# Trainium2: a hybrid attention, mLSTM and convolution layer: another issue order in the first quarter, another ring for the residual loads, other durations in the order's estimate

## The chip, the cores and the metric

One core of one Trainium2 chip runs the whole kernel. TensorE (PE) does matmuls and transposes, VectorE (DVE), ScalarE (ACT) and GpSimd (POOL) the elementwise work, and every transfer is issued by one DMA queue, that of SyncE (SP). The metric is the time of one execution on the device in microseconds (us), over which the median of several runs is taken.

## The reference

x is 2048 tokens by 1024 channels, and there is one layer. One input projection feeds three groups, and one output projection mixes them and adds the residual:

```python
h = rms_norm(x, norm_g)
a_q, a_k, a_v, a_z, m_q, m_k, m_v, m_o, m_z, m_i, m_f, c_a, c_b, c_z = split_columns(h @ w_in)

att = chunk_band_attention(a_q, a_k, a_v, ...)         # 4 heads of 64, chunks of 64 tokens, 8 chunks back
att = att * silu(a_z)

m_q, m_k = silu(causal_depthwise_conv([m_q, m_k], width 4))
hm = mlstm_chunkwise(m_q, m_k, m_v, m_i + b_i, m_f + b_f)   # 4 heads of 128, state carried over tokens
ml = rms_norm(sigmoid(m_o) * hm) * silu(m_z)

u = c_a * sigmoid(c_b)                                  # 256 channels
u = causal_depthwise_conv(u, width 31)
cv = silu(layer_norm(u)) * silu(c_z)

out = x + concat(att, ml, cv) @ w_out
```

## The kernel before, in words

The sequence is worked in four quarters of 512 tokens (`NQ`, `TQ`). In each quarter every projection is a *unit*: `kv`, `qg` (queries and gate inputs), `v`, `o`, then `mk`, `mq`, `z` of mLSTM heads 0 to 3, `az` and `cz` (gates of attention and convolution), `cb` and `ca` (inputs of the convolution), and `out0` to `out7`. A unit with the tokens along the free side (`cm`) is 24 matmuls of 128x512: 8 blocks of channels times 3 passes, since each product is made of rounded high and low parts. A unit like `v` has 96 of them. Names in a row tell the unit: `pmm_az` is the PSUM bank of an `az` unit.

In the first quarter a piece of weights comes raw (`rw`), ACT casts it and POOL (sometimes DVE) makes the low part (`w<-rw,w`); the pair is kept in DRAM (`wk`) and later quarters load it from there (`w<-wk`). The ring of weight tiles has 10 (`WB`).

The small work hangs on *chains*, Python generators that emit instructions on all engines. While the program of a unit is written, the chains that are due are advanced between its matmuls. What is due is decided by an estimate: `Engine`, `dma`, `mm` and `tp` keep a clock for each engine, and `pace`, `tick` and `wait_for` read it. The estimate fixes the order of instructions once, when the kernel is built. On the chip each engine runs its own list in that order, and so does the DMA queue, in which a transfer that must wait holds back those behind it. The list of units is fixed by hand: `FIRST` + `TAIL` for quarter 0, `LATER` + `TAIL` for the others, and eight `out` units of the last quarter at the end (`order_of`). The `out` units of a quarter run at the head of the next quarter's list.

Chains that the prediction speaks of:
- the gates chain: from the eight gate inputs (`gt`) VectorE makes log-sigmoids with a polynomial of eight small steps (`gpp<-gpp,gz`); then PE transposes the result (`ptg<-ident_r,gt`), while `v` units fill PE;
- a head of the mLSTM: after `mk` and `mq`, four taps of a short convolution on DVE (`macc<-mraw,mcw_t,macc` three times, and `macc<-mraw,macc` behind the SiLU), then transposes `pk`, scores `pS<-macc`, and for each of four blocks three products `pp` (numerator with `kw`, with `dt`, and with the state `cst`);
- the attention: scores `pss`, softmax on DVE (`pr<-pss`), transposes `ptp`, products `po`;
- the convolution: 62 taps a quarter on DVE (`cvu<-cvu,cvw_t`), and behind the last tap the layer norm by blocks (`ptl` on PE, `bst`, `bmv` and `cvu<-ptl,bmv,brs` on DVE, `brs` on POOL), then transposes back (`pty`);
- the gates `az`, `z`, `cz` (`gate`, `att_gate`), two to three DVE steps behind each unit;
- the next quarter's input: x comes transposed in eight pieces (`xk<-in_xT`), DVE scales one (`xk<-xk,gx,rb`), ACT rounds it, DVE makes the low part (`xT<-xk,xT`); the first `cb` unit of the quarter reads the eight pairs in turn;
- the end of an `out` unit (`finish`): the residual `xr` (`fetch_x`, `fetching`), an addition on DVE (`xr<-pmm_out,xr`), a store.

SBUF slots are rings by tag (`SLOTS`): X, W, H, A, B and others; a chain that wants a slot waits for the oldest of that ring.

Of the kernel before, what the change touches and what calls it, by code (L numbers as in the profile page):

```python
# [10 lines left out]
F32R = mybir.dt.float32r  # L11
# [4 lines left out]
P = 128  # L16
S = 2048
D = 1024
# [10 lines left out]
LAG = 4  # L29
DEPTH = 3  # L30

SLOTS = {"X": (5, 512), "W": (4, 528), "H": (5, 512), "A": (2, 512), "M": (1, 516), "Q": (1, 768), "B": (2, 256), "R": (3, 640),
         "T": (2, 640)}
TAP = 1.0
SEM = 0.12
# [4 lines left out]
        + [("qg", TM, 4), ("v", TM, 8), ("o", TM, 8)]  # L40
        + [(f"{n}{h}", CM, 2) for n in ("mk", "mq", "z") for h in range(4)]
        + [(f"{n}{j}", CM, 2) for n in ("az", "cz") for j in range(2)] + [(f"out{i}", CM, 2) for i in range(8)])
FIRST = ["kv", "cb0", "ca0", "cb1", "ca1", "qg", "v", "mk0", "mq0", "o", "mk1", "mq1"]
LATER = ["out0", "out1", "out2", "out3", "cb0", "ca0", "kv", "out4", "cb1", "ca1", "qg", "out5", "v", "mk0", "mq0", "o",
         "out6", "mk1", "mq1", "out7"]
TAIL = ["z0", "mk2", "mq2", "z1", "mk3", "mq3", "az0", "az1", "z2", "cz0", "cz1", "z3"]
KIND = {n: k for n, k, _ in PLAN}
PIECES = {}
_at = 0
# [5 lines left out]


def order_of(q):
    return [f"out{i}" for i in range(8)] if q == NQ else (LATER if q else FIRST) + TAIL


LOG = None
# [3 lines left out]
def kernel(ctx: ExitStack, tc: tile.TileContext, x, xT, wp, wq, norm_g, qg, kg, bias, far,  # L65
# [3 lines left out]

    free = {"V": 0.0, "A": 0.0, "G": 0.0, "D": 0.0}  # L70
    wrote, read, grain = {}, {}, {}

    class Pool:

# [171 lines left out]
    class Engine:  # L246
# [3 lines left out]
        def __getattr__(self, name):  # L250
            fn = getattr(self.eng, name)

            def call(*a, **k):
                i = tc.keep_in_program_order(fn(*a, **k))  # L254
                aps = [v for v in a if isap(v)]
                out_ = [k["out"]] if "out" in k else aps[:1]
                aps = aps if "out" in k else aps[1:]
                acc = [k["accum_out"]] if isap(k.get("accum_out")) else []
                ins = aps + [v for n_, v in k.items() if n_ not in ("out", "accum_out") and isap(v)]
                n = max([size(ap) for ap in out_ + ins if not any(st_ == 0 for st_, c_ in ap.ap[1:])] or [1])  # L260
                two = sum(1 for ap in ins if size(ap) * 2 > n) > 1 or any(ap.space == bass.MemoryType.PSUM for ap in ins)
                if self.key == "A":
                    d = 0.17 + 0.00085 * n + 0.1 * isap(k.get("scale")) + 0.08 * isap(k.get("bias")) + 0.19 * bool(acc)
                elif self.key == "V":
                    d = (0.16 + 0.00104 * n if two else 0.14 + 0.00056 * n) + 0.09 * bool(acc)
                    d += 0.05 * any(isap(k.get(x)) for x in ("scalar", "scalar1", "scalar2"))
                elif k.get("op") == ALU.pow:
                    d = 1.0
                else:
                    d = 0.25 + (0.0021 * n if two else 0.0)  # L270
                end = max(free[self.key], rdy(*ins), busy(*out_)) + d
                free[self.key] = end
                for ap in ins:
                    was_read(ap, end)
                for ap in out_ + acc:
                    was_written(ap, end + SEM)
                return i
            return call
# [3 lines left out]
    def dma(out, in_):  # L282
        start = max(clk["t"], rdy(in_), busy(out), free["D"])
        free["D"] = start + 4 * size(out) * out.shape[0] / 330e3
        was_read(in_, free["D"] + 1.0)
        was_written(out, free["D"] + 2.2)
        tc.keep_in_program_order(nc.sync.dma_start(out=out, in_=in_))

    def stall(t, what):
# [12 lines left out]

    def mm(out_, lhsT, rhs, start, stop, share=1.0):
        n = size(rhs)
        run_pe(out_, (lhsT, rhs), 0.006 + 0.00043 * n if lhsT.dtype == F32R else share * 2 * (0.004 + n / 1200.0))
        tc.keep_in_program_order(PE.matmul(out_, lhsT=lhsT, rhs=rhs, start=start, stop=stop))  # L306

    def tp(out_, in_, n=P):
        rnd = in_.dtype == F32R
        run_pe(out_, (in_,), 0.062 if rnd else 0.11)  # L310
        tc.keep_in_program_order(PE.transpose(out=out_, in_=in_, identity=(ident_r if rnd else ident)[0:n, 0:n]))  # L311


# [248 lines left out]

    def x_block(b, t, rs, xt):
        yield (rs[:, b:b + 1],)
        dg = yield from take("dg", P)
        A.activation(out=dg, in_=ident, func=AF.Copy, scale=rs[:, b:b + 1])
        yield (dg,)
        c = slice(b * P, (b + 1) * P)
        for hk in range(2):
            xb = (yield from take("xb", 512)).rearrange("p (a b) -> p a b", a=4)  # L570
            yield from bank_wait()
            pt, pt_ = bank("pxt")
            for k in range(4):
                mm(pt[:, k, :], t[:, (4 * hk + k) * P:(4 * hk + k + 1) * P], dg, True, True)
            ks = slice(4 * hk, 4 * hk + 4)
            V.tensor_tensor(out=xb, in0=pt, in1=gx[:, ks].unsqueeze(2).to_broadcast([P, 4, P]), op=ALU.mult)
            shut(pt_)
            yield (xb,)
            A.copy(out=xt[:, 0, ks, c], in_=xb)
            yield (xt[:, 0, ks, c],)  # L580
            V.tensor_tensor(out=xt[:, 1, ks, c], in0=xb, in1=f(xt[:, 0, ks, c]), op=ALU.subtract)
            drop(xb)
        drop(dg)
        done.add((0, b))
# [98 lines left out]
        return cs  # L683

    def q_chain(q, b, ps, gt, items, deps):
        raw = yield from take("qr", 256, tag="B")
        A.copy(out=raw, in_=ps[:, 0:256])
        V.tensor_tensor(out=gt[:, :, b], in0=ps[:, 256:264], in1=gb_t, op=ALU.add)
        ps_done(ps)
        box["gt"] = box.get("gt", 0) + 1  # L690
        yield from norm_heads(raw, "q")
        n3 = raw.rearrange("p (h d) -> p h d", d=64)
        V.tensor_tensor(out=n3, in0=n3, in1=gqk.unsqueeze(1).to_broadcast([P, 4, 64]), op=ALU.mult)
        yield (raw,)
        stk = (yield from take("qstk", 768, F32R, "Q")).rearrange("p (a b) -> p a b", a=4)
        A.copy(out=stk[:, :, 0:64], in_=n3)
        yield (stk,)
        V.tensor_tensor(out=stk[:, :, 64:128], in0=n3, in1=f(stk[:, :, 0:64]), op=ALU.subtract)
        V.tensor_copy(out=stk[:, :, 128:192], in_=f(stk[:, :, 0:64]))
        drop(raw)  # L700
        yield (stk,)
        while not all(c["done"] for c in deps) or len(items) > 5:
            yield 0.3
        qT = []
        for v_ in range(2):
            t = (yield from take(f"qT{v_}", 512, F32R)).rearrange("p (a b) -> p a b", a=4)
            yield from bank_wait()
            pt, pt_ = bank("ptq", F32R)
            for h in range(4):
                tp(pt[:, h, :], stk[:, h, 64 * v_:64 * v_ + P])  # L710
            A.copy(out=t, in_=pt)
            shut(pt_)
            qT.append(t)
        drop(stk)
        items.extend([(b, h, qT) for h in range(4)])
# [446 lines left out]


    def out_unit(i):
        fetch_x(i)
        ps = cm(box["mt"][0], f"out{i}", box["mt"][2])
        step(spawn(finish(i, ps, box["mt"][1])))

    def fetch_x(i):
        spawn(fetching(i, box["mt"][1]))  # L1170

    def fetching(i, q):
        xr = yield from take("xr", 512)
        yield max(0.0, busy(xr) - clk["t"])
        dma(out=xr, in_=xT[i * P:(i + 1) * P, q * TQ:(q + 1) * TQ])
        box["xr", q, i] = xr
# [7 lines left out]
    for q in range(NQ):  # L1184
# [129 lines left out]
```

## Time and profile before

| | |
|---|---|
| Median of 3 runs | 1225.51 us (1222.08 to 1225.66) |
| Profiled execution, its own time | 1225.23 us |
| Its span, first to last instruction | 1223.5 us |
| Granted TensorE clock, mean | 0.987 of full speed |
| PE / DVE / ACT / POOL busy | 96% / 65% / 35% / 20% of the span |
| Bytes moved | 240.25 MB, 196 GB/s over the span |

Some 1.7 us of the execution's time lie outside its span. A busy share tells how long an engine had something to do; an engine's idle time matters only if the chain of work that ended last runs through it. Here PE has 48.3 us of idle time in all, so the views to read are the one that names what PE waited for, and the one that gives busy time stretch by stretch.

### The profile page before, as it was taken

What the parts mean: (1) busy time and instruction counts of PE and PEld (TensorE: products, weight loads), DVE (VectorE), ACT (ScalarE), POOL (GpSimd) and SP (SyncE); (2) the same over time, 40 slices, a digit from 0 to 9 for tenths busy, and PEclk for the clock granted to TensorE, in tenths of its full rate; (3) what the DMA queues carried; (4) which work ended last, traced back from release to release, by engine and by line L of the source; (5) the groups of instructions that cost most, each with busy time, mean ns of one, the idle gap of its engine ahead of it and who ended that gap; (6) DMA issues with size and microseconds to landing.
All of it is one profiled execution on the core that took longest, in us unless ns stands there. A gap on an engine that the chain in (4) does not pass through costs nothing.

```text
span 1223.5 us, 17647 instructions
## 1 busy us (share of the span) xinstructions
PE 1175.2 (96%) x6308; PEld 967.1 (79%) x6308; DVE 797.7 (65%) x1845; ACT 430.3 (35%) x984; POOL 244.9 (20%) x325
## 2 busy tenths in 40 slices
PE   6988996999999999999899999999999999999998
PEld 5776775777778888888678888888877888888886
DVE  6386897985567577775456666767537666677731
ACT  4454633443323441334232343233312244223320
POOL 5572543560222011110022100001002200010200
PEclk9998998999999999999999999999999999999999
DMA  9583856767673417655936351855674615275463
GB/s 354 187 312 118 313 175 240 240 219 266 234 277 121 176 67 259 206 158 170 325 109 238 122 191 35 289 178 170 195 266 152 223 46 208 91 255 187 154 218 111
DMA packets 95408, 240.25 MB, mean 196 GB/s; under 512 B 11288, under 2 KB 28248, under 8 KB 95320
## 3 DMA queue, kind: packets, MB, share of 16 engines
q1 hardware_dynamic: 95320, 239.11, 57.2%
q8 instruction: 50, 0.82, 0.3%
q14 instruction: 38, 0.31, 0.1%
HBM read 186.52 MB, written 52.56 MB: 195 GB/s over the span
## 4 chain that ended last, share of the span: by engine, by line
PE 79%; DVE 9%; DMA 5%; POOL 3%; issue 2%; ACT 2%; SPq 0%; POOLq 0%; ACTq 0%; DVEq 0%
PE pmm_out L306 12%; PE pmm_v L306 7%; PE pmm_o L306 7%; PE pmm_mk L306 6%; PE pmm_mq L306 6%; PE pmm_z L306 6%; PE pmm_cz L306 4%; PE pp L306 3%; PE pmm_kv L306 3%; PE pmm_az L306 3%; PE po L306 3%; PE pmm_qg L306 3%; PE pmm_ca L306 3%; PE pss L306 3%; DVE cvu L254 3%; PE ptp L311 3%
## 5 line engine op out<-in xcount | busy, mean ns | idle before, releaser
L254 DVE SCALAR_TENSOR_TENSOR cvu<-cvu,cvw_t 128x512 f32<-128x512 f32 x240 | 193.1, 805 | 10.6 <-ACT cvu L254 6.9
L306 PE MATMUL pmm_out<-mT,w 128*128 128x512 f32 x768 | 189.2, 397 | 1.4 <-ACT mT L254 1.2
L306 PEld LDWEIGHTS pmm_out<-mT,w 128*128 128x128 f32 x768 | 141.6, 188 | 31.6 <-ACT mT L254 1.4
L254 POOL TENSOR_TENSOR w<-rw,w 128x512 fp32r<-128x512 f32 (+1 forms) x80 | 116.2, 1467 | 183.6 <-ACT w L254 180.7
L306 PE MATMUL pmm_v<-w,xT 128*128 128x512 f32 x384 | 113.4, 417 | 0.6 <-POOL w L254 0.6
L306 PE MATMUL pmm_mk<-xT,w 128*128 128x512 f32 x384 | 104.5, 405 | 0.0
L306 PE MATMUL pmm_z<-xT,w 128*128 128x512 f32 x384 | 99.8, 404 | 0.0
L306 PE MATMUL pmm_mq<-xT,w 128*128 128x512 f32 x384 | 98.2, 400 | 0.0
L306 PE MATMUL pmm_o<-w,xT 128*128 128x512 f32 x384 | 97.7, 401 | 0.0
L306 PE MATMUL pmm_kv<-w,xT 128*128 128x512 f32 x384 | 94.5, 401 | 0.0
L254 DVE SCALAR_TENSOR_TENSOR macc<-mraw,mcw_t,macc 128x512 f32<-128x512 f32 x96 | 84.0, 875 | 7.7 <-ACT macc L254 5.4
L306 PEld LDWEIGHTS pmm_kv<-w,xT 128*128 128x128 f32 x384 | 72.2, 191 | 16.3 <-ACT xT L254 0.2
L306 PEld LDWEIGHTS pmm_o<-w,xT 128*128 128x128 f32 x384 | 70.2, 188 | 15.3 <-issue 1.0
L306 PEld LDWEIGHTS pmm_mq<-xT,w 128*128 128x128 f32 x384 | 70.5, 189 | 14.8 <-issue 0.9
L306 PEld LDWEIGHTS pmm_z<-xT,w 128*128 128x128 f32 x384 | 70.8, 191 | 13.9
L306 PEld LDWEIGHTS pmm_mk<-xT,w 128*128 128x128 f32 x384 | 69.4, 189 | 13.3 <-issue 0.7
L306 PEld LDWEIGHTS pmm_v<-w,xT 128*128 128x128 f32 x384 | 68.2, 192 | 13.6 <-issue 2.1
L254 POOL COPY mch<-mraw 128x3 f32<-128x3 f32 x32 | 10.2, 319 | 297.1 <-ACT mraw L254 296.8
L306 PE MATMUL pmm_cb<-xT,w 128*128 128x512 f32 x192 | 50.4, 409 | 8.7 <-ACT xT L254 7.1
L254 ACT CAST w<-rw 128x512 fp32r<-128x512 f32 (+1 forms) x80 | 48.5, 618 | 26.7 <-DMA rw<-in_wp 8.1
L254 DVE TENSOR_TENSOR xr<-pmm_out,xr 128x512 f32<-128x512 f32 x32 | 22.0, 689 | 54.4 <-PE pmm_out L306 31.9
L254 ACT COPY pT<-ptp 128x384 f32<-128x384 f32 (+2 forms) x64 | 29.4, 459 | 73.4 <-PE ptp L311 72.9
(231 smaller groups left out, 1995.3 us busy)
## 6 DMA issues: line engine op xcount, KB each, us to landing
w<-wk SPq DMA_DIRECT2D x240, 512.0 KB, 4.2
wk<-w SPq DMA_DIRECT2D x80, 512.0 KB, 5.6
rw<-in_wp SPq DMA_DIRECT2D x80, 256.0 KB, 4.6
xr<-in_xT SPq DMA_DIRECT2D x32, 256.0 KB, 5.1
out<-xr SPq DMA_DIRECT2D x32, 256.0 KB, 4.8
xbig<-in_x SPq DMA_DIRECT2D x14, 512.0 KB, 7.2
w<-wk SPq DMA_DIRECT2D x12, 528.0 KB, 7.6
xk<-in_xT SPq DMA_DIRECT2D x24, 256.0 KB, 5.5
```

The costliest lines, as they stand in the source:

```text
L254: i = tc.keep_in_program_order(fn(*a, **k))
L306: tc.keep_in_program_order(PE.matmul(out_, lhsT=lhsT, rhs=rhs, start=start, stop=stop))
L311: tc.keep_in_program_order(PE.transpose(out=out_, in_=in_, identity=(ident_r if rnd else ident)[0:n, 0:n]))
```

## The change

Five things are edited.

1. `FIRST` becomes the whole list of quarter 0. Its end has `az0` and `az1` between the heads; the two `cz` units stand ahead of `z2` and `z3`. `TAIL` is now that of quarters 1 to 3, with `mk2` and `mq2` ahead of `z0` and `mk3`, `mq3` ahead of `z1`.
2. Tag B has three slots in place of two; the diagonal tile `dg` and the last `qr` of a quarter come from tag A.
3. The residual `xr` of quarters 1 to 3 comes from tag W in place of X, and is fetched one `out` unit earlier. For quarter 0 it stays in X and in its own unit.
4. The estimate gets other durations: of matmuls, of transposes, of a transfer's landing, and of DVE instructions that overlap a large POOL instruction.
5. With that, the points at which chains are advanced move in all quarters. The matmuls are the same ones in number and shape, as are the instructions of the other engines.

```diff
-SLOTS = {"X": (5, 512), "W": (4, 528), "H": (5, 512), "A": (2, 512), "M": (1, 516), "Q": (1, 768), "B": (2, 256), "R": (3, 640),
+SLOTS = {"X": (5, 512), "W": (4, 528), "H": (5, 512), "A": (2, 512), "M": (1, 516), "Q": (1, 768), "B": (3, 256), "R": (3, 640),
-FIRST = ["kv", "cb0", "ca0", "cb1", "ca1", "qg", "v", "mk0", "mq0", "o", "mk1", "mq1"]
+FIRST = ['kv', 'cb0', 'ca0', 'cb1', 'ca1', 'qg', 'v', 'mk0', 'mq0', 'o', 'mk1', 'mq1', 'az0', 'z0', 'mk2', 'mq2', 'az1', 'z1', 'mk3', 'mq3', 'cz0', 'cz1', 'z2', 'z3']
-TAIL = ["z0", "mk2", "mq2", "z1", "mk3", "mq3", "az0", "az1", "z2", "cz0", "cz1", "z3"]
+TAIL = ['mk2', 'mq2', 'z0', 'mk3', 'mq3', 'z1', 'az0', 'az1', 'z2', 'cz0', 'cz1', 'z3']
 def order_of(q):
-    return [f"out{i}" for i in range(8)] if q == NQ else (LATER if q else FIRST) + TAIL
+    return [f"out{i}" for i in range(8)] if q == NQ else LATER + TAIL if q else FIRST
+    slow = {"G": (0.0, 0.0)}
-                end = max(free[self.key], rdy(*ins), busy(*out_)) + d
+                start = max(free[self.key], rdy(*ins), busy(*out_))
+                if self.key == "G" and n > 64:
+                    slow["G"] = (start, start + d)
+                elif self.key == "V" and not any(ap.space == bass.MemoryType.PSUM for ap in ins):
+                    d += 0.75 * max(0.0, min(slow["G"][1], start + d) - max(slow["G"][0], start))
+                end = start + d
     def dma(out, in_):
-        was_read(in_, free["D"] + 1.0)
-        was_written(out, free["D"] + 2.2)
+        was_read(in_, free["D"] + 2.2)
+        was_written(out, free["D"] + 3.0)
     def mm(out_, lhsT, rhs, start, stop, share=1.0):
-        run_pe(out_, (lhsT, rhs), 0.006 + 0.00043 * n if lhsT.dtype == F32R else share * 2 * (0.004 + n / 1200.0))
+        run_pe(out_, (lhsT, rhs), 0.006 + 0.00044 * n if lhsT.dtype == F32R else share * 2 * (0.0046 + n / 1200.0))
     def tp(out_, in_, n=P):
-        run_pe(out_, (in_,), 0.062 if rnd else 0.11)
+        run_pe(out_, (in_,), 0.085 if rnd else 0.111)
     def x_block(b, t, rs, xt):
-        dg = yield from take("dg", P)
+        dg = yield from take("dg", P, tag="A")
     def q_chain(q, b, ps, gt, items, deps):
-        raw = yield from take("qr", 256, tag="B")
+        raw = yield from take("qr", 256, tag="A" if b == NB - 1 else "B")
     def out_unit(i):
-        fetch_x(i)
+        if box["mt"][1] == 0:
+            fetch_x(i)
+        elif i + 1 < KT:
+            fetch_x(i + 1)
     def fetching(i, q):
-        xr = yield from take("xr", 512)
+        xr = yield from take("xr", 512, tag="W" if q else "X")
         box["heads"] = heads
+        if q:
+            fetch_x(0)
```

Three places show how instructions move.

The first is PE in quarter 0, at the scores `pS` of mLSTM head 1, behind its unit `mq1`. The `pp` triple ahead of `pS` is the last block of head 0, that behind it the first of head 1. Before:

```order
L306 MATMUL pmm_mq_1953<-xT_122,w_1815 128x512 x11
L306 MATMUL pp<-vt,kw 128x129
L306 MATMUL pp<-vt,dt 128x129
L306 MATMUL pp<-cst_115,iw 128x129
L311 MATMUL pk<-ident_r,macc 128x128 x4
L306 MATMUL pS<-macc 128x128 x4
L306 MATMUL pmm_z_2077<-xT_122,w_1823 128x512 x5
L306 MATMUL pp<-vt,kw 128x129
L306 MATMUL pp<-vt,dt 128x129
L306 MATMUL pp<-cst_116,iw 128x129
```

In the changed kernel:

```order
L311 MATMUL pmm_mq_1951<-xT_122,w_1815 128x512 x10
L311 MATMUL pmm_az_2009<-xT_122,w_1823 128x512 x12
L311 MATMUL pmm_az_2009<-xT_122,w_1834 128x512 x12
L311 MATMUL pp<-vt,kw 128x129
L311 MATMUL pp<-vt,dt 128x129
L311 MATMUL pp<-cst_115,iw 128x129
L316 MATMUL pk<-ident_r,macc 128x128 x4
L311 MATMUL pS<-macc 128x128 x4
L311 MATMUL pmm_z_2121<-xT_122,w_1878 128x512 x4
L311 MATMUL pp<-vt,kw 128x129
L311 MATMUL pp<-vt,dt 128x129
L311 MATMUL pp<-cst_116,iw 128x129
```

The 24 matmuls of `az0` now stand between the end of `mq1` and `pS`; before, only three `pp` and four `pk` stood there.

The second is PE at the end of quarter 0, with the layer norm's four transposes of two (`ptl`), the last two blocks of head 3 (`pp`) and the transposes of a head's output (`pto`). Before:

```order
L311 MATMUL ptl<-ident_r,cvu 128x128 x2
L306 MATMUL pmm_cz_2705<-xT_122,w_2388 128x512 x5
L311 MATMUL pto<-ident_r,og 128x128 x4
L306 MATMUL pp<-vt,kw 128x129
L306 MATMUL pp<-vt,dt 128x129
L306 MATMUL pp<-cst_118,iw 128x129
L306 MATMUL pmm_cz_2705<-xT_122,w_2388 128x512 x4
L306 MATMUL pmm_cz_2705<-xT_122,w_2432 128x512 x10
L311 MATMUL ptl<-ident_r,cvu 128x128 x2
L306 MATMUL pmm_cz_2705<-xT_122,w_2432 128x512 x2
L306 MATMUL pmm_cz_2792<-xT_122,w_2453 128x512 x11
L311 MATMUL ptl<-ident_r,cvu 128x128 x2
```

In the changed kernel:

```order
L316 MATMUL ptl<-ident_r,cvu 128x128 x2
L311 MATMUL pmm_z_2708<-xT_122,w_2429 128x512 x3
L311 MATMUL pp<-vt,kw 128x129
L311 MATMUL pp<-vt,dt 128x129
L311 MATMUL pp<-cst_118,iw 128x129
L311 MATMUL pmm_z_2708<-xT_122,w_2429 128x512
L316 MATMUL ptl<-ident_r,cvu 128x128 x2
L311 MATMUL pp<-vt,kw 128x129
L311 MATMUL pp<-vt,dt 128x129
L311 MATMUL pp<-cst_118,iw 128x129
L316 MATMUL pto<-ident_r,og 128x128 x4
L316 MATMUL ptl<-ident_r,cvu 128x128 x2
```

Before, 19 and 13 matmuls of 128x512 stand between the second, third and fourth `ptl`; now it is four between the second and the third, and between the third and the fourth only a block's `pp` and a head's `pto`.

The third is the DMA queue at the end of quarter 1, from the fifth (before) or the sixth (changed) of the eight pieces of the next quarter's x (`xk`) on. Before:

```order
L287 DMA xk<-in_xT 128x512
L287 DMA w_5800<-wk_192 128x1024
L287 DMA xk<-in_xT 128x512
L287 DMA w_5822<-wk_214 128x1024
L287 DMA xk<-in_xT 128x512
L287 DMA xr<-in_xT 128x512
L287 DMA out<-xr 128x512
L287 DMA w_5843<-wk_226 128x1024
L287 DMA w_5861<-wk_259 128x1024
L287 DMA xbig<-in_x 128x1024 x2
L287 DMA xk<-in_xT 128x512
L287 DMA out<-xr 128x512
```

In the changed kernel:

```order
L292 DMA xr<-in_xT 128x512
L292 DMA xk<-in_xT 128x512
L292 DMA out<-xr 128x512
L292 DMA w_5807<-wk_198 128x1024
L292 DMA xk<-in_xT 128x512
L292 DMA w_5827<-wk_224 128x1024
L292 DMA xk<-in_xT 128x512
L292 DMA xr<-in_xT 128x512
L292 DMA out<-xr 128x512
L292 DMA w_5850<-wk_226 128x1024
L292 DMA w_5868<-wk_258 128x1024
L292 DMA xbig<-in_x 128x1024 x2
```

The eighth and last piece (the `xk` nearest the end of each list) stood behind two pieces of weights and the two halves of `xbig`; now it stands ahead of the last two pieces and of `xbig`. The end of quarter 2 has the same turn without `xbig`.

## Rows read from the trace of the kernel before

**Rows 1.** Waits of PE: what waited, for what, us in total, times, longest.

```profile
PE pS L306 <- DVE macc L254: 12.5, 6, 7.6
...
PE pmm_cb L306 <- ACT xT L254: 7.1, 5, 3.6
...
PE ptg L311 <- DVE gt L254: 3.8, 1, 3.8
...
PE pmm_cb L306 <- DVE xT L254: 1.6, 4, 0.9
...
PE pmm_out L306 <- ACT mT L254: 1.2, 1, 1.2
```

**Rows 2.** Windows: stretch, length, busy us of each engine, PE clock, DMA share, GB/s.

```profile
0.00:282.00 282.00, 250.94 (x1307) 204.43 (x1308) 213.80 (x430) 131.49 (x301) 143.68 (x154) 0.96 0.67 239
...
582.00:613.00 31.00, 25.66 (x109) 19.71 (x107) 13.02 (x20) 7.68 (x13) 0.00 (x0) 0.94 0.95 322
...
613.00:881.00 268.00, 267.41 (x1489) 221.80 (x1490) 176.64 (x447) 90.71 (x213) 30.16 (x56) 0.99 0.50 167
...
881.00:910.00 29.00, 26.46 (x115) 20.56 (x113) 13.78 (x22) 5.64 (x10) 0.00 (x0) 1.00 0.91 307
```

**Rows 3.** Timeline of PE, quarter 0 and quarter 2: start, us, instruction.

```profile
97.41 2.05 PE L306 MATMUL pmm_v<-w,xT 128*128 128x512 f32 x4
...
650.66 5.69 PE L306 MATMUL pmm_cb<-xT,w 128*128 128x512 f32 x24
```

**Rows 4.** Timeline of DVE, the gates chain in quarter 0.

```profile
92.18 4.51 DVE L254 SCALAR_TENSOR_TENSOR gpp<-gpp,gz 128x16 f32<-128x16 f32 x7
...
96.73 0.17 DVE L254 SCALAR_TENSOR_TENSOR gpp<-gpp,gz__934 128x16 f32<-128x16 f32 x1
...
97.14 0.17 DVE L254 SCALAR_TENSOR_TENSOR gt<-gpp,gz__934 128x16 f32<-128x16 f32 x1
```

**Rows 5.** Timeline of POOL beside the gates chain.

```profile
90.84 4.98 POOL L254 TENSOR_TENSOR w<-rw,w 128x512 fp32r<-128x512 f32 x4 [1.00 <-ACT w L254]
```

**Rows 6.** Timeline of PE, scores of head 1 and of head 3, quarter 0.

```profile
194.38 2.08 PE L306 MATMUL pS<-macc 128*128 128x128 f32 x8 [7.60 <-DVE macc L254]
...
196.11 2.48 PE L306 MATMUL pmm_z<-xT,w 128*128 128x512 f32 x5
...
252.00 1.16 PE L306 MATMUL pS<-macc 128*128 128x128 f32 x8 [1.40 <-DVE macc L254]
```

**Rows 7.** Timeline of DVE, the two steps behind a unit `az`.

```profile
251.86 0.67 DVE L254 SCALAR_TENSOR_TENSOR az<-az,pmm_az 128x512 f32<-128x512 f32 x1
252.57 1.08 DVE L254 SCALAR_TENSOR_TENSOR ao<-az,ao 128x512 f32<-128x512 f32 x1
```

**Rows 8.** Windows of quarter 0, columns as in the windows above.

```profile
150.00:200.00 50.00, 40.05 (x186) 33.06 (x185) 43.38 (x68) 16.79 (x36) 21.70 (x19) 0.90 0.65 228
200.00:260.00 60.00, 56.50 (x289) 46.84 (x288) 53.21 (x100) 27.57 (x65) 31.89 (x28) 1.00 0.64 215
```

**Rows 9.** Timeline of DVE, one block of the layer norm.

```profile
273.16 0.43 DVE L254 BATCH_NORM_STATS2 bst<-ptl 128x6 f32<-128x256 f32 x1 [0.55 <-PE ptl L311]
...
274.76 0.54 DVE L254 TENSOR_SCALAR cvu<-ptl,bmv,brs 128x256 f32<-128x256 f32 x1 [0.95 <-POOL brs L254]
```

**Rows 10.** Timeline of PE, the first units of quarter 2.

```profile
612.94 1.95 PE L306 MATMUL pmm_cb<-xT,w 128*128 128x512 f32 x3 [3.61 <-ACT xT L254]
614.69 2.48 PE L306 MATMUL pmm_ca<-xT,w 128*128 128x512 f32 x7
```

**Rows 11.** Timeline of SP's queue, the last piece of x for quarter 2.

```profile
603.35 0.53 SPq L287 DMA_DIRECT2D xk<-in_xT  x1
```

**Rows 12.** Timeline of DVE at the head of quarter 2.

```profile
605.23 0.69 DVE L254 TENSOR_TENSOR xr<-pmm_out,xr 128x512 f32<-128x512 f32 x1 [3.53 <-DMA xr<-in_xT]
...
611.49 0.75 DVE L254 SCALAR_TENSOR_TENSOR xk<-xk,gx,rb 128x512 f32<-128x512 f32 x1 [2.93 <-DMA xk<-in_xT]
```

**Rows 13.** Window over the attention of quarter 2.

```profile
673.00:747.00 74.00, 74.00 (x484) 60.92 (x483) 48.94 (x176) 31.59 (x72) 3.98 (x9) 1.00 0.41 143
```

More of the change, by code (lines that the diff above doesn't have):

```diff
@@ L42 @@
         + [(f"{n}{j}", CM, 2) for n in ("az", "cz") for j in range(2)] + [(f"out{i}", CM, 2) for i in range(8)])
-FIRST = ["kv", "cb0", "ca0", "cb1", "ca1", "qg", "v", "mk0", "mq0", "o", "mk1", "mq1"]
-LATER = ["out0", "out1", "out2", "out3", "cb0", "ca0", "kv", "out4", "cb1", "ca1", "qg", "out5", "v", "mk0", "mq0", "o",
-         "out6", "mk1", "mq1", "out7"]
-TAIL = ["z0", "mk2", "mq2", "z1", "mk3", "mq3", "az0", "az1", "z2", "cz0", "cz1", "z3"]
+FIRST = ['kv', 'cb0', 'ca0', 'cb1', 'ca1', 'qg', 'v', 'mk0', 'mq0', 'o', 'mk1', 'mq1', 'az0', 'z0', 'mk2', 'mq2', 'az1', 'z1', 'mk3', 'mq3', 'cz0', 'cz1', 'z2', 'z3']
+LATER = ['out0', 'out1', 'out2', 'out3', 'cb0', 'ca0', 'kv', 'out4', 'cb1', 'ca1', 'qg', 'out5', 'v', 'mk0', 'mq0', 'o', 'out6', 'mk1', 'mq1', 'out7']
+TAIL = ['mk2', 'mq2', 'z0', 'mk3', 'mq3', 'z1', 'az0', 'az1', 'z2', 'cz0', 'cz1', 'z3']
 KIND = {n: k for n, k, _ in PLAN}
```

## The prediction

> **What bounds the kernel now.** I first read the waits of PE, then windows by quarter, then the timelines at the waits that are long. PE is busy 96% of the span and its work is the same in both kernels, so the time can change in two ways only: PE waits less or more, or its clock is lower for a shorter or longer time. The windows say where: quarter 0 up to 282 us lacks 282.00 - 250.94 = 31.1 us of PE; the head of quarter 2 (582 to 613) lacks 5.3, the head of quarter 3 (881 to 910) lacks 2.5, and the 268 us of quarter 2 between them only 0.6 [rows 2]. The waits name the causes: the scores `pS` behind the short convolution `macc` 12.5 us, the first `cb` units behind `xT` 7.1 + 1.6, the transposed gates `ptg` 3.8, the first `out` of a quarter behind `mT` 1.2 [rows 1]. The start of the program, which the change hardly touches, holds most of the rest. So the change has some 28 us of waits within reach, and the quarters 1 to 3, where it moves most instructions, have nothing to give, only to lose.
>
> A wait also costs clock. Behind the wait for `ptg`, four matmuls of 128x512 took 2.05 us, where 24 in quarter 2 take 5.69, or 0.24 each [rows 3]; behind the `pS` of head 1, eight `pS` took 2.08 and five `z` 2.48, where eight `pS` behind a wait of 1.40 took 1.16 [rows 6]. The clock was 0.90 over 150 to 200 us and 1.00 over 200 to 260 [rows 8], though that stretch holds another wait of 1.4 us. So the long waits are followed by matmuls at half rate, and short ones are not.
>
> **A: the gates chain in quarter 0.** In PE's list 21 `v` matmuls stand ahead of `ptg`; now 31 do. Ten more at 0.24 are 2.4 us of work that PE does while it would have waited. The chain's own end also comes earlier: the third B slot and the A slot let the last block's queries begin sooner, and its `gt` stands seven rows earlier in DVE's list; I estimate 1.9 us. Sum -4.2, more than the wait of 3.8 because shorter waits ahead of it shrink as well. The bounds: 2.3 if the chain ends where it did; 5.5 if shorter waits on the way fall too. Seven small DVE steps took 4.51 us there, one alone 0.17 [rows 4], and POOL made four subtractions in the same stretch in 4.98 [rows 5]. The Trainium skill, SBUF — State Buffer, section Who interferes with whom, says that a DVE instruction with two SBUF inputs and a GpSimd one that reads SBUF exclude each other, and that the later is held for the whole of the other. The rows agree: 0.64 a step is not 0.17, and POOL kept its 1.25. By that rule 0.75 of the overlap is too little for a small step, and `gt` would come no earlier; A would be -2.3.
>
> **B: `pS` of head 1.** Ahead of it now stand 24 matmuls of `az0`: 24 x 0.24 = 5.7 us of work in a wait of 7.6 [rows 3, 6]. On DVE the two steps behind `az` stand ahead of the last `macc`: 0.67 + 1.08 [rows 7], and one tap of 0.75 less. So `macc` ends 0.3 to 1.0 later and 4.5 to 5.4 us are won: -5.0. For heads 2 and 3 units stand in the same way between `mq` and `pS`; their waits were 2.1 and 1.4 of the 12.5 [rows 1]. I take -2.5 of these 3.5, with 1.5 to 3.5 as bounds.
>
> **Clock in quarter 0.** At half rate the stretch behind `pS` of head 1 lost 2.08 - 1.16 + 2.48 - 5 x 0.24, that is 2.2, and some 0.8 in the `pp` between; the stretch behind `ptg` lost 2.05 - 4 x 0.24 = 1.1 and some 0.5 after [rows 3, 6]. Together 4.6. If what is left of the waits is 2 us or less, it comes back. I take -2.5, between 0 and 4.6.
>
> **D: the end of quarter 0.** This loses. The `cz` units, which stood between the layer norm's `ptl`, are spent earlier, and the last tap ends later. One block of the layer norm needs from `bst` 273.16 to the end of `cvu` at 275.30, that is 2.1 us, until its PSUM bank is free [rows 9]; there are two banks. Between the third and the fourth `ptl` now stand only one `pp` triple and a `pto`, about 1 us, between the second and third four matmuls. So I expect some 2.9 of waiting at the fourth `ptl`, 1.0 at the last `pp`, 0.6 at `pto` and 0.5 at `pty`: +5.0. The first `out` waits less for `mT`, since the units that feed it come earlier: -1.1 of 1.2 [rows 1]. Together +3.9. Bounds: 0, if the taps end as early as before; +6.5, if no work lies between any of them.
>
> **E: heads of quarters 2 and 3.** Before, the last `xk` left the queue at 603.35 [rows 11], landed for a DVE step at 611.49, and PE went on at 612.94 [rows 10, 12]. DVE, which works in order, also stood 3.53 us at an `xr` addition for a residual still on its way [rows 12]. Now the residuals are loaded a unit earlier, and two weight pieces and two halves of `xbig` no longer stand ahead of the last `xk`, with one store: 4 x 0.52 + 0.26 = 2.36 MB. At the 322 GB/s of that stretch [rows 2] they are 7.3 us. The last `xk` then lands at 604 and its product is ready at about 605.6; PE without its waits wants it at 612.94 - 5.3 = 607.6. So the waits go: -5.3 and -2.5 [rows 2]. The clock too: three `cb` took 1.95 and seven `ca` 2.48 [rows 10], at 0.24 each 0.7 and 1.7, a loss of 2.0; at quarter 3 I take the same, an estimate. Sum -11.8; I take -11 for a remnant. Bounds -5 (the eighth piece still half late at both) and -12. Quarter 1's head has no prefetch and stays.
>
> **F: what stands closer elsewhere.** In quarters 1 to 3 the new durations advance attention chains faster, about 65 us of PE work in quarter 2 where it was 74. DVE was busy 48.94 of 74 us there [rows 13]; 48.94 of 65 is 75%, so I expect only strays: +2 (0 to 6), over all quarters. The earlier transfers of `xr` lie in slots of W that are free by then; cost nothing, and if not, `finish` waits as it did before. Diagonal tiles and `qr` in tag A: nothing, under the start's waits, which stay.
>
> **Sum** against the profiled execution's 1225.23 (0.3 below the median of the runs): -4.2 - 5.0 - 2.5 - 2.5 + 3.9 - 11 + 2 = -19.3, so 1205.9.
>
> **Rivals.**
> 1. *VectorE is the bound of quarter 0.* It was busy 43.38 of 50 us and 53.21 of 60 [rows 8], and the change takes no work off it. Then PE meets the same wait one step later: A gives 2.3, B 3, heads 2 and 3 and the clock nothing, D costs 5, F 2. Against it: 13.4 us of these 110 are idle, more than the 7.5 that B and its followers need. -2.3 - 3 + 5 + 2 - 11 = -9.3, so 1216. For it: small steps of DVE took 0.64 in place of 0.17 us beside POOL [rows 4], and POOL is at work in half of these stretches [rows 8]. By the Trainium skill's rule above, steps of `macc` would stretch in the same way.
> 2. *The heads of quarters stay late.* DMA is busy 0.95 there [rows 2], so a piece that leaves earlier may only share the same bytes' time. Against it: fewer bytes stand ahead. Without E -8.3, so 1217; with half of it 1211.
> 3. *Slower: attention starves in quarters 1 to 3.* 48 blocks of a head in three quarters; each has PE wait for a softmax of DVE. To eat 19.3 us and 3.7 more, each must wait 0.48 us. Then 1229. The point from which it decides: DVE would need over 4.1 us a block (65 / 16), where it was busy 48.94 / 16 = 3.1 [rows 13]. So it is unlikely.
> 4. *Nothing comes of it:* gains and D cancel, 1223 to 1227.
>
> **Chances.** Forecast 0.55 (own range 1198 to 1212), rival 1 0.20, rival 2 0.11, nothing 0.08, slower 0.06. A measurement of this kernel can tell about 0.3%, or 3.7 us, from no change. Faster: the first three, less a little for their far ends, 0.84; same 0.10; slower 0.06. The range reaches over the rivals 1 and 2 on the upper side, and to the clock and A at their best on the lower: 1196 to 1221.
>
> **What would show it.** A: the wait at `ptg` under 1 us. B: `pS` of head 1 waits 1 to 3 us, in place of 7.6, and matmuls behind it at 0.24. D: new waits at `ptl`, in the last 15 us of quarter 0, of 3 to 5 us in sum. E: the windows at the two heads with PE full, no `cb` waiting, the last `xk` some 7 us earlier. F: no row for `pss` or `ptp` above 3 us in the waits. It is wrong if `pS` still waits over 5 us, if `ptl` and its followers wait over 7, or if `cb` at quarter 2 waits over 2.

## The result

| | before | changed |
|---|---|---|
| Median of 4 runs each | 1224.88 us | 1210.53 us (1208.68 to 1214.34) |
| Ratio, 95% interval | | 0.9891 (0.9860 to 0.9922) |
| Profiled execution, its span | 1225.23, 1223.5 | 1211.88, 1210.1 |

The change makes the kernel 1.1% faster. The forecast of 1206 us had the direction and the range (1196 to 1221) right; of the 19.3 us in its sum the profile shows 13.4. Below, "changed kernel" is the one of the diff.

The windows of the changed kernel, in the same stretches as [rows 2] and with the same columns:

```profile
0.00:282.00 282.00, 253.14 (x1307) 206.60 (x1308) 211.27 (x429) 132.18 (x301) 143.52 (x154) 0.97 0.68 240
...
582.00:613.00 31.00, 30.77 (x133) 24.68 (x132) 14.37 (x21) 8.70 (x15) 0.00 (x0) 1.00 0.94 333
613.00:881.00 268.00, 267.69 (x1502) 222.69 (x1501) 179.72 (x453) 92.50 (x215) 31.17 (x55) 1.00 0.50 173
881.00:910.00 29.00, 29.00 (x127) 23.56 (x126) 13.65 (x21) 5.14 (x8) 0.21 (x1) 1.00 0.83 285
```

PE is full in the two windows of the heads: 30.77 of 31 us and 29.00 of 29, where 25.66 and 26.46 were. (The windows stand at the same times in both traces; quarter 3's first `out` begins 8.5 us earlier in the changed kernel.) Quarter 0 gained only 2.2 us of PE's busy time, and the reader should not take that for 2.2 us won, as matmuls at a low clock are busy too. The waits of PE, as in [rows 1]:

```profile
PE pS L311 <- DVE macc L254: 5.5, 2, 4.9
PE ptp L316 <- DVE pr L254: 3.3, 1, 3.3
...
PE pmm_ca L311 <- DVE xr L254: 1.9, 1, 1.9
...
PE ptl L316 <- DVE gz L254: 1.7, 1, 1.7
PE pmm_out L311 <- DVE xr L254: 1.7, 1, 1.7
...
PE pmm_out L311 <- DVE mT L254: 1.1, 3, 0.6
PE pp L311 <- DVE og L254: 1.0, 1, 1.0
```

No `cb` waits any more. `pS` waits 5.5 us in place of 12.5. But other waits are new or stand at new places: 3.3 at `ptp`, now for a softmax step of VectorE behind the gates chain; 1.7 at `ptl`; 1.0 at the `pp` of the last block of quarter 0 (before, a `pp` waited 1.7 elsewhere); and 1.7 for `xr` at an `out`. The rows left out in the fence hold more of quarter 0, such as 2.0 at `pss` (0.4 before) and 1.2 at a `pk`.

Idle time alone doesn't add up to the difference. What does is the time at which PE begins each unit, read from its timeline in both traces. Lengths in us; in the third and fourth stage the changed kernel has two `cz` units earlier, so 48 matmuls are moved back at 5.55 a unit (the distance of two full units in the fence for term E below):

| Stage | before | changed | difference | foreseen |
|---|---|---|---|---|
| start to `v` of quarter 0 | 81.8 | 81.6 | -0.2 | 0 |
| `v` to `mk0` (A) | 45.6 | 46.7 | +1.1 | -4.2 |
| `mk0` to `z2` (B, heads 2 and 3, clock) | 128.6 | 131.7 - 11.1 | -8.0 | -10.0 |
| `z2` to `kv` of quarter 1 (D) | 64.4 | 60.0 + 11.1 | +6.7 | +3.9 |
| heads of quarters 2 and 3, first `out` to `kv` (E) | 42.7 + 39.9 | 35.2 + 35.2 | -12.2 | -11 |
| the rest of quarters 1 to 3 (F) | 771.3 | 770.3 | -1.0 | +2 |
| last `out` units | 49.2 | 49.4 | +0.2 | 0 |

So the gain is that of the heads of quarters 2 and 3, and quarter 0 comes out even, as near as one profile of each can tell. Two runs below show how near that is. E2 has the changed kernel's order of instructions on every engine until past 570 us, and its `kv` of quarter 1 begins at 316.4 us, where the changed kernel's begins at 320.0. E1 has that of the kernel before for as long, and begins it at 318.1 where the kernel before has 320.4. The four stages of quarter 0 are therefore good to some 2 to 4 us in sum. A little work also crosses the borders of the stages: eight `ptq` (0.7 us) now stand behind the beginning of `v`, and one block's `pp` (0.6 us) behind that of `z2`. Without them the differences are +0.5, +0.4, -7.4 and +6.1.

### The profile page after: what moved, and what is told of

Same layout as the page of the kernel before. It is cut to its first block, busy times and chain, and to the rows that moved or that the text cites. A ratio compares the mean times of both kernels' runs of the same rounds, so it can differ in the third digit from the quotient of the medians.

```text
span 1210.1 us, 17636 instructions
## 1 busy us (share of the span) xinstructions
PE 1172.0 (97%) x6308; PEld 968.1 (80%) x6308; DVE 794.8 (66%) x1845; ACT 432.7 (36%) x984; POOL 248.7 (21%) x325
## 4 chain that ended last, share of the span: by engine, by line
PE 83%; DVE 6%; DMA 4%; POOL 3%; issue 3%; ACT 1%; SPq 0%; POOLq 0%; ACTq 0%; DVEq 0%
PE pmm_out L311 13%; PE pmm_v L311 7%; PE pmm_z L311 7%; PE pmm_mk L311 7%; PE pmm_mq L311 6%; PE pmm_kv L311 6%; PE pmm_o L311 6%; PE pmm_cz L311 4%; PE pp L311 3%; PE pmm_qg L311 3%; PE po L311 3%; PE pmm_ca L311 3%; PE pss L311 3%; PE pmm_az L311 3%; PE ptp L316 3%
## 5 line engine op out<-in xcount | busy, mean ns | idle before, releaser
L311 PEld LDWEIGHTS pmm_out<-mT,w 128*128 128x128 f32 x768 | 141.8, 188 | 34.7 <-DVE mT L254 2.5
L254 DVE SCALAR_TENSOR_TENSOR macc<-mraw,mcw_t,macc 128x512 f32<-128x512 f32 x96 | 79.4, 827 | 7.5 <-ACT macc L254 5.1
L311 PE MATMUL pmm_az<-xT,w 128*128 128x512 f32 x192 | 49.7, 401 | 0.0
```

## The experiments

### Who makes the gain at the heads of the quarters

E1 is the kernel before with the residual edit alone:

```diff
 def out_unit(i):
-    fetch_x(i)
+    if box["mt"][1] == 0:
+        fetch_x(i)
+    elif i + 1 < KT:
+        fetch_x(i + 1)
 ...
-    xr = yield from take("xr", 512)
+    xr = yield from take("xr", 512, tag="W" if q else "X")
 ...
+    if q:
+        fetch_x(0)
```

> The kernel before with the residual edit alone (xr of quarters 1 to 3 in tag W, one out unit ahead); lists, slots and estimate as before. Theory 1 (the whole gain is the heads of quarters 2 and 3, and the residual edit makes it): the cb waits of 5.3 and 2.5 us go, ratio 0.989 to 0.992, 1212 to 1215 us. Rival (the estimate's new transfer durations pull the last piece of x forward): the waits stay and the time is 1224.

Measured: 1214.35 us, 0.9911 (0.9896 to 0.9925). From the first `out` to `kv` its heads take 34.7 and 35.4 us (42.7 and 39.9 before), and `cb` has no row in its waits. Theory 1 holds; the estimate has no part in it. The interval overlaps that of the changed kernel (0.9860 to 0.9922): these runs can't tell that the other four edits add anything to this one.

E2 is the changed kernel with that diff undone.

> The changed kernel with the residual edit undone alone (xr in tag X, fetched in its own unit). Up to the end of quarter 1 its lists are those of the changed kernel. Theory 1: cb waits at the heads of quarters 2 and 3 come back, 8 to 12 us in all with the clock, 1219 to 1223 us. Rival (the estimate does it): 1210 to 1212.

Measured: 1228.83 us, 1.0034 (1.0017 to 1.0052): 0.3% slower than before, and further than was expected. The waits are back, as PE's timeline of E2 shows at the head of quarter 2:

```profile
610.00 1.95 PE L311 MATMUL pmm_cb<-xT,w 128*128 128x512 f32 x3 [2.65 <-ACT xT L254]
611.75 6.54 PE L311 MATMUL pmm_ca<-xT,w 128*128 128x512 f32 x19
```

These heads take 44.8 and 40.3 us, a little more than before. With E1 this settles that the residual edit is needed and enough for term E. Its two halves, the other ring and the fetch one unit earlier, were not run apart. In the program, `xr` and `xk` both took slots of tag X before, so the ring alone may have held back the last `xk`; which half does it is not shown. Why E2 ends above the kernel before can't be read from its trace: the profiled execution was with 1224.68 the shortest of its five.

### What the new list is worth

E3 puts the old end of the list back into the changed kernel's quarter 0:

```diff
-FIRST = [..., 'mk1', 'mq1', 'az0', 'z0', 'mk2', 'mq2', 'az1', 'z1', 'mk3', 'mq3', 'cz0', 'cz1', 'z2', 'z3']
+FIRST = [..., 'mk1', 'mq1', 'z0', 'mk2', 'mq2', 'z1', 'mk3', 'mq3', 'az0', 'az1', 'z2', 'cz0', 'cz1', 'z3']
```

> The changed kernel with the old list of quarter 0 (z0, mk2, mq2, z1, mk3, mq3, az0, az1, z2, cz0, cz1, z3 at its end), all else as changed. Theory 1 (the new list wins some 8 us at the scores of heads 1 to 3 and loses as much at the layer norm): 1208 to 1213 us, with pS of head 1 waiting 6 to 8 us again and no ptl waiting. Rival (the list is a net gain of 5 or more that other edits eat): 1215 to 1218.

Measured: 1216.66 us, 0.9933 (0.9911 to 0.9954), with `pS` of head 1 waiting 8.4 us and no `ptl`. The rows are those of theory 1, the time is that of the rival: beside the changed kernel's 0.9891 the list is worth some 0.4%, though the intervals overlap. The trace of E3 puts its loss past the layer norm: from the first `out` of quarter 0 to `kv` of quarter 1 it takes 42.8 us (38.3 in the changed kernel, 36.9 in E2 with the same list), with 2.9 us of waiting for `mT`.

E12 is the kernel before with the residual edit and both lists, but the old estimate and slots.

> The kernel before with the residual edit and the two lists, with the old estimate and slots. Theory (lists and residuals carry the gain, the estimate and slots add nothing beyond a few us either way): 1207 to 1211 us. Rival (the lists need the new durations to pay): 1213 to 1218.

Measured: 1212.47 us, 0.9911 (0.9895 to 0.9928), just above what the first theory allows and below the rival's: no more than E1 has without the lists. So the lists pay only with the estimate and slots, if at all, and neither helps alone beyond what these runs can tell.

E8 takes the overlap term out of the estimate (0.75 becomes 0.0):

> The changed kernel with 0.75 set to 0 in the estimate: DVE's instructions cost the same beside a large POOL instruction. Theory 2 says that the term stands for something real, so without it PE's lists put consumers ahead of what DVE can deliver: waits at pS of over 8 us in sum, 1214 to 1220 us. Rival (the term moves little that matters): 1208 to 1212.

Measured: 1219.93 us, 0.9966 (0.9954 to 0.9978). `pS` waits 8.3 us and `pk` 3.1, and a `cb` of quarter 1 waits 4.4 (0.6 in the kernel before). The time is that of theory 2, but by itself it doesn't show that the term stands for something real: E6 below loses as much, with the same wait at `cb`, by a change of the list alone. What the term stands for is shown by E4 and E5.

### What holds VectorE in quarter 0

E4 changes the POOL instruction that makes the low part of a weight piece, and nothing in any engine's order (the edit is shortened here):

```diff
-G.tensor_tensor(out=w[:, 1], in0=raw, in1=f(w[:, 0]), op=ALU.subtract)
+nc.gpsimd.memset(f(w[:, 1]), 0.0)      # booked in the estimate as the subtraction was
```

> The changed kernel with the low part of quarter 0's weights left out: where POOL subtracted, it fills with zeros, at the same place in every engine's list; POOL then only writes. Theory 2 (DVE steps with two SBUF inputs are shut out while POOL reads): the seven gpp take 1.2 us in place of 4.5, ptp behind them stops waiting, the macc of heads 1 to 3 take 0.75 each, pS of head 1 waits under 3 us; 1199 to 1205 us. Rival (the steps are slow for another reason, such as waits between them): gpp stay near 0.6 each and the time is 1208 to 1212.

Measured: 1192.19 us, 0.9727 (0.9709 to 0.9745), a larger gain than was expected. PE's, VectorE's, ScalarE's and SyncE's instructions stand in the same order in both traces. VectorE's timeline in the gates chain, and POOL's beside it:

```profile
84.69 2.13 DVE L254 TENSOR_SCALAR gpp<-gz 128x16 f32<-128x16 f32 x1
86.85 1.43 DVE L254 SCALAR_TENSOR_TENSOR gpp<-gpp,gz 128x16 f32<-128x16 f32 x7
```

```profile
83.94 2.85 POOL L454 MEMSET w<- 128x512 f32 x6
```

The seven steps take 1.43 us, 0.20 each. But a fill is shorter than a subtraction (0.48 us against 1.25), and here the last of them ended at 86.79, just before the first of the seven steps: POOL was idle beside them, so E4 alone can't tell its reading from its being busy. E5 fills each piece three times:

> As the kernel without POOL's reads (low part of quarter 0's weights left out), but POOL fills each piece three times, so that it is busy some 1.4 us a piece as with the subtraction's 1.25, and still reads nothing. Theory 2 (what shuts DVE out is POOL's reading): the seven gpp take under 2 us, 1191 to 1198 us. Rival (it is POOL's busy time, whatever it does): gpp back at 4 us or more, 1206 to 1212 us.

Measured: 1195.43 us, 0.9764 (0.9730 to 0.9797). VectorE and POOL again:

```profile
85.67 0.38 DVE L254 TENSOR_SCALAR gpp<-gz 128x16 f32<-128x16 f32 x1
86.08 1.43 DVE L254 SCALAR_TENSOR_TENSOR gpp<-gpp,gz 128x16 f32<-128x16 f32 x7
```

```profile
84.92 9.95 POOL L455 MEMSET w<- 128x512 f32 x18
```

POOL is busy for 10 us on end, all through the seven steps, and they still take 1.43. So it is not POOL's time that counts, it is its reading. All of the gain lies in quarter 0: `kv` of quarter 1 begins at 301.0 us in E4 and at 303.1 in E5. A fill also doesn't wait for the raw piece, so the low parts are ready earlier; what that is worth was not run apart, but in the changed kernel PE waited only 1.2 us in all for low parts of POOL. The groups of DVE instructions up to 285 us (count, busy us and mean ns), first of the changed kernel:

```profile
L254 DVE SCALAR_TENSOR_TENSOR cvu<-cvu,cvw_t 128x512 f32<-128x512 f32 x60 | 56.8, 947 | 2.2 <-ACT cvu L254 1.4
L254 DVE SCALAR_TENSOR_TENSOR macc<-mraw,mcw_t,macc 128x512 f32<-128x512 f32 x24 | 24.5, 1023 | 0.7
```

and of E5:

```profile
L254 DVE SCALAR_TENSOR_TENSOR cvu<-cvu,cvw_t 128x512 f32<-128x512 f32 x60 | 44.8, 748 | 2.2 <-ACT cvu L254 1.4
L254 DVE SCALAR_TENSOR_TENSOR macc<-mraw,mcw_t,macc 128x512 f32<-128x512 f32 x24 | 18.0, 750 | 0.7
```

Over the whole run VectorE is busy 794.8 us in the changed kernel and 752.5 in E5. The 42.3 us between them, over the 80 subtractions of the whole run, are 0.53 us a piece.

E9 lets VectorE make the eight low parts of unit `v` itself (0.68 us each), and E10 four of them. Both start from E7 (below):

```diff
-(V if j < 8 and j % 2 == 0 else G).tensor_tensor(...)
+(V if j < 8 and j % 2 == 0 or 20 <= j < 28 else G).tensor_tensor(...)
```

> The kernel with the residual edit for quarter 0 too, and the low parts of the eight weight pieces of unit v in quarter 0 made by VectorE in place of POOL. Theory 2 (a POOL subtraction shuts DVE out for 1.25 us in the gates chain, DVE's own would take 0.7): the seven gpp take under 2 us, the first ptp and ptg wait under 1 us, 2 to 4 us less than the 1207 of its parent, 1203 to 1205. Rival (the eight subtractions of 5.5 us fill DVE as much as the lock did): 1206 to 1209.

> As the one with v's low parts on VectorE, but only four of the eight. Theory 2: between that one and its parent, 1204 to 1206. Rival: as the parent, 1206 to 1209.

E11 cuts POOL's subtraction into four of 128 columns, for the same eight pieces:

> The kernel with the residual edit for quarter 0 too, and POOL's subtraction for v's eight pieces cut into four of 128 columns. Theory 2 (DVE is held until the running POOL instruction ends): a small DVE step waits a quarter as long, the seven gpp take 1.5 to 2.5 us, and the time is 1203 to 1206. Rival (the fixed part of more POOL instructions makes v's weights late): PE waits longer for w, 1208 or more.

Measured: E9 1217.54 us, 0.9950 (0.9936 to 0.9965); E10 1214.24, 0.9925 (0.9910 to 0.9940); E11 1210.92, 0.9898 (0.9883 to 0.9912). By their medians all three are slower than E7. In E11 the mechanism did what it should:

```profile
88.47 2.51 DVE L254 SCALAR_TENSOR_TENSOR gpp<-gpp,gz 128x16 f32<-128x16 f32 x7
```

The seven steps fell to 2.51 us, and the first `out` of quarter 0 began at 275.4 us, 4.4 earlier than in E7. Behind that the three lost it again: in PE's timeline of E11

```profile
285.65 1.95 PE L311 MATMUL pmm_out<-mT,w 128*128 128x512 f32 x3 [3.20 <-ACT mT L254]
290.02 20.12 PE L311 MATMUL pmm_out<-mT,w 128*128 128x512 f32 x75 [2.42 <-ACT mT L254]
```

the first `out` waits twice for `mT`, and from there to `kv` of quarter 1 it takes 45.7 us where E7 takes 36.4; E9 and E10 take 46.1 and 46.5. In E11's list the last `ptl` and all `pty` stand behind the beginning of the first `out`; E9 and E10 have the same waits for `mT`, 5.6 us in sum. All three runs have other lists from about the beginning of unit `v` on, as the estimate books other durations, so these waits can't be put down to POOL or VectorE alone. E9 also has a new wait, for a low part that stands in VectorE's list behind the gates chain:

```profile
94.16 1.22 PE L311 MATMUL pmm_v<-w,xT 128*128 128x512 f32 x2 [5.33 <-DVE w L254]
```

So both theories are missed as to the time. What theory 2 says of the mechanism holds in E9 and E11 (the seven steps took 1.43 and 2.51 us); in E10 the first `ptp` still waits 3.7 us.

### The end of quarter 0, and a better version

E6 moves `az1` back so that the two `cz` units stand between the layer norm's blocks again:

```diff
-[..., 'az0', 'z0', 'mk2', 'mq2', 'az1', 'z1', 'mk3', 'mq3', 'cz0', 'cz1', 'z2', 'z3']
+[..., 'az0', 'z0', 'mk2', 'mq2', 'z1', 'mk3', 'mq3', 'az1', 'z2', 'cz0', 'cz1', 'z3']
```

> The changed kernel with another end of quarter 0's list: az0, z0, mk2, mq2, z1, mk3, mq3, az1, z2, cz0, cz1, z3. Theory 3 (the loss of 6 to 7 us at the layer norm comes from the two cz units being spent ahead of it): no wait at ptl and pp there, pS of head 1 as in the changed kernel, 1203 to 1207 us. Rival (VectorE is the bound of quarter 0, so the waits only turn up at pS of heads 2 and 3 or at the first out): 1209 to 1213 us.

Measured: 1221.04 us, 0.9973 (0.9961 to 0.9986). At `ptl` only 0.5 us is left, but two `pp` wait 2 us each, and quarter 1's input is late:

```profile
319.62 1.95 PE L311 MATMUL pmm_cb<-xT,w 128*128 128x512 f32 x3 [4.62 <-ACT xT L254]
```

Neither theory: theory 3 fails, since the `pp` still wait with the `cz` units back between the blocks, and the rival named other places.

E7 gives quarter 0's residuals the same treatment as the others (`tag="W"`, `fetch_x(0)` and `fetch_x(i + 1)` in every quarter).

> The changed kernel with the residual edit for quarter 0 too (tag W, one unit ahead). Theory: the waits for xr at the outs of quarter 0, 1.7 and 1.9 us, go: 1206 to 1209 us. Rival (another wait ends there next, or W's slots are not free): 1210 to 1212.

Measured: 1207.21 us, 0.9861 (0.9838 to 0.9884), as expected. No wait for `xr` is left, and the first `out` to `kv` of quarter 1 takes 36.4 us in place of 38.3. But E2 took 36.9 there without this edit, with 0.3 us of waiting at the same `out`, so that part of the gain isn't shown. It is the fastest version with all of the computation; 3 us from the changed kernel, with intervals that overlap.

## Why the prediction was right, and where its sizes were off

The time came into the range because term E is most of the gain: E was foreseen at -11 and measured at -12.2, and all the rest at -8.3 and measured at -1.2. The measured 1210.5 lies about midway between the forecast (1206) and rival 1 (1216), so the time alone doesn't choose between them; the stages do.

**E, foreseen -11, measured -12.2.** Right in mechanism, place and size. SP's queue of the changed kernel, then VectorE, then PE at the head of quarter 2:

```profile
597.28 0.38 SPq L292 DMA_DIRECT2D xk<-in_xT  x1
...
599.88 2.87 SPq L292 DMA_DIRECT2D w<-wk  x2
602.80 0.90 SPq L292 DMA_DIRECT2D xbig<-in_x  x2
```

```profile
602.57 0.69 DVE L254 TENSOR_TENSOR xr<-pmm_out,xr 128x512 f32<-128x512 f32 x1
...
604.32 0.75 DVE L254 SCALAR_TENSOR_TENSOR xk<-xk,gx,rb 128x512 f32<-128x512 f32 x1 [0.28 <-DMA xk<-in_xT]
```

```profile
602.23 5.72 PE L311 MATMUL pmm_cb<-xT,w 128*128 128x512 f32 x24
607.78 5.72 PE L311 MATMUL pmm_ca<-xT,w 128*128 128x512 f32 x24
```

The last `xk` left at 597.28 us, 6.1 us before the time in [rows 11], ahead of two weight pieces and `xbig`. VectorE took it at 604.32, where the prediction had it land at 604; in [rows 12] that was 611.49. The `xr` addition at 602.57 waits for no transfer. PE runs two units in 5.55 us each, at full rate, where [rows 10] show 0.65 us a matmul. Rival 2 (shared bytes) falls: the DMA share is 0.94 and 0.83 in these windows, and the data are in time all the same. What is shown is the edit (E1, E2) and the place in the queue; that the two weight pieces and `xbig` cost the last `xk` just the 7.3 us of the prediction's estimate was not run apart.

**A, foreseen -4.2, measured +1.1.** This step failed. (Its parts, 2.4 and 1.9, add to 4.3.) E2, E3, E6 and E7, whose lists are the same up to there, have 44.3, 45.8, 45.8 and 44.4 us for the stage, so between -1.3 and +1.1, 0.7 of it for the `ptq` that moved in: nothing. VectorE, POOL and PE of the changed kernel:

```profile
92.46 4.47 DVE L254 SCALAR_TENSOR_TENSOR gpp<-gpp,gz 128x16 f32<-128x16 f32 x7
...
97.39 0.17 DVE L254 SCALAR_TENSOR_TENSOR gt<-gpp,gz__937 128x16 f32<-128x16 f32 x1
...
98.47 0.29 DVE L254 TENSOR_SCALAR pr<-pr,li 128x128 f32<-128x128 f32 x1
```

```profile
88.62 6.27 POOL L254 TENSOR_TENSOR w<-rw,w 128x512 fp32r<-128x512 f32 x5
95.64 1.26 POOL L254 TENSOR_TENSOR w<-rw,w 128x512 fp32r<-128x512 f32 x1 [0.75 <-PE pmm_v L311]
```

```profile
98.90 0.45 PE L316 MATMUL ptp<-ident_r,pr 128*128 128x128 f32 x1 [3.33 <-DVE pr L254]
...
100.31 0.63 PE L316 MATMUL ptg<-ident_r,gt 128*16 128x128 f32 x2
```

The ten more matmuls did run ahead of `ptg`. What failed is the estimate that the chain ends 1.9 us earlier: `gt` began at 97.39, at 97.14 in [rows 4], since the steps ran again beside POOL's subtractions. And PE did not get the 2.4 us of the matmuls: the softmax `pr`, which stands behind the chain in VectorE's list, ended only at 98.76, so PE waited 3.33 at `ptp` in place of 3.77 at `ptg`. In the kernel before, the first softmax stood ahead of the chain, and PE had waited for it earlier:

```profile
89.52 0.30 PE L311 MATMUL ptp<-ident_r,pr 128*128 128x128 f32 x1 [2.04 <-ACT pr L254]
```

The prediction looked at `ptg` alone and passed over this `ptp`, which stood behind 15 `v` matmuls and now stands behind 29. Those 2.04 us are gone, but two waits at `pss` grew from 0.4 to 2.0 us and `v` waited 0.6 us longer for low parts, so PE's idle time in the stage went from 7.0 to 6.5 us only. So the wait changed its name, and the two `v` behind `ptp` took 1.20 us, about half rate, as the four in the kernel before with 2.05 [rows 3]. The cause is shown by the same seven steps: 4.47 us here, 1.43 in E4 and E5, and 2.51 in E11. The Trainium skill, SBUF — State Buffer, section Who interferes with whom, has it: only the GpSimd instruction that reads SBUF excludes a DVE instruction with two SBUF inputs, and one that only writes does not. These runs agree, at 0.64 us a step beside reads and 0.20 beside writes. In the prediction the page's -2.3 came nearer than the -4.2 that was taken, and was still too good, as it left out what is queued behind the chain.

**B, heads 2 and 3, clock, foreseen -10.0, measured -8.0.** Right in mechanism, wrong in its parts, and near in sum partly by luck. PE, then VectorE:

```profile
184.50 5.68 PE L311 MATMUL pmm_az<-xT,w 128*128 128x512 f32 x24
...
196.24 1.81 PE L311 MATMUL pS<-macc 128*128 128x128 f32 x8 [4.95 <-DVE macc L254]
197.70 2.05 PE L311 MATMUL pmm_z<-xT,w 128*128 128x512 f32 x4
```

```profile
192.51 0.68 DVE L254 SCALAR_TENSOR_TENSOR az<-az,pmm_az 128x512 f32<-128x512 f32 x1
193.22 1.29 DVE L254 SCALAR_TENSOR_TENSOR ao<-az,ao 128x512 f32<-128x512 f32 x1
194.43 1.75 DVE L254 SCALAR_TENSOR_TENSOR macc<-mraw,macc 128x512 f32<-128x512 f32 x1
```

`az0` ran in 5.68 us ahead of `pS`. The wait fell from 7.60 only to 4.95, or by 2.65 where 5.0 was foreseen, as the last `macc` took 1.75 where 0.68 to 0.75 was assumed, again beside a subtraction of POOL. `az0` also filled a wait that the prediction had not counted, at the `pp` just ahead of `pk` and `pS`, which is gone in the changed kernel:

```profile
185.35 0.46 PE L306 MATMUL pp<-vt,kw 128*128 128x129 f32 x2 [1.74 <-DVE og L254]
```

In E2, E6 and E7, with the same list up to there, `pS` waited 5.4, 7.0 and 7.2 us; so this term varies by 2 us with how the two engines fall together, and by the prediction's own sign (wrong if `pS` still waits over 5) it just holds here and fails in those three. The clock did not come back at this place: the four `z` behind `pS` took 2.05 us. Heads 2 and 3 gave 1.7 us where 2.5 was foreseen, within the bounds: of 3.5 us, 0.6 at `pS` and 1.2 at `pk` are left. The waits of the stage fell by 6.1 us and 0.6 is the block of `pp` that moved out; that leaves some 1.3 for the clock and all else, where 2.5 was foreseen for the clock.

**D, foreseen +3.9, measured +6.7.** The places were right:

```profile
269.39 0.46 PE L311 MATMUL pp<-vt,kw 128*128 128x129 f32 x2 [1.05 <-DVE og L254]
...
272.76 0.69 PE L316 MATMUL ptl<-ident_r,cvu 128*128 128x128 f32 x2 [1.70 <-DVE gz L254]
273.11 4.62 PE L311 MATMUL pmm_z<-xT,w 128*128 128x512 f32 x10
...
303.25 5.82 PE L311 MATMUL pmm_out<-mT,w 128*128 128x512 f32 x24 [1.67 <-DVE xr L254]
```

The last `pp` waits 1.05 (1.0 foreseen), the fourth `ptl` 1.70 (2.9 foreseen). `pto` and `pty`, 1.1 in the sum, have no wait. Two things had no price in it: the ten `z` behind them took 4.62 us, 2.2 above full rate, and a wait of 1.67 for `xr` at an `out` of quarter 0. The prediction gave back the clock that shorter waits return, and charged none for the new ones: it had read from its rows that short waits are not followed by matmuls at half rate, and here a wait of 1.70 was (0.46 us a matmul). In E2, with the same list and the same two waits of 1.05 and 1.70, the ten `z` took 3.72 us, the `out` waited 0.3 for `xr`, and the stage came out at +4.0. So how much of the +6.7 is the order, and how much differs from one execution to the next, is open between +4.0 and +6.7.

**F, foreseen +2, measured -1.0.** The waits at `pss` and `ptp` all lie in quarter 0; the attention of quarters 1 to 3 has none. Rival 3 falls.

**Rival 1** (VectorE is the bound of quarter 0) is the nearest to what came in quarter 0: no net gain there, by the same wait one step later. E4 and E5 bear it out: without POOL's reads, and in the same order, the ratio to the kernel before falls by another 1.3 to 1.6 points, all of it in quarter 0. Its time (1216) was too high because B and heads 2 and 3 won more than it allowed, and F cost nothing.

Open stays why the residual edit is worth more in the changed kernel (E2) than in the one before (E1), and how much of E3's and E12's small differences is chance.

## What to carry to other kernels

A wait of the bounding engine is not removed by putting work ahead of the waiter, if the one it waits for is late through its whole list: look at what stands behind the late instruction on its own in-order engine, and name the next waiter before counting the gain. The stalls at the heads of quarters 2 and 3 were a matter of what stood ahead in the one DMA queue; loads that may start earlier, in a ring that has room, brought the heads to 35 us under both lists and both estimates (E1, E12, the changed kernel). And an order that an estimate writes reacts as a whole: E6, E9 and E11 each mended the wait that they aimed at and lost the gain again a few stages on. A stage of one profile is worth a comparison with a second run of the same order before its microseconds are added up: here quarter 0 differed by up to 4 us between two such runs.

## What the runs showed of the hardware

VectorE lost 0.53 us for each of the 80 POOL subtractions of 128x512 and 128x528, 42 us in all, and its taps lost nothing to a POOL fill that only writes (the `cvu` and `macc` groups at 748 and 750 ns in E5, 947 and 1023 in the changed kernel). One kind of step was held even beside fills: the single `TENSOR_SCALAR` that opens the chain took 2.13 us in E4 and 0.38 in E5, and 0.17 in E9, where POOL was idle at that time. The same list gave a `pS` wait between 4.95 and 7.2 us in four kernels, so a wait of some microseconds in one profile is no exact size.
